# Memory values multiplied by the output weights ahead of the attention, 1/Z moved into the residual addition, and the down projection's first loads moved

## The chip, the cores and the metric

The kernel runs on one core of a Trainium2 chip. Its time is the device time of one execution in microseconds (us); the median of several runs counts. The engines are TensorE (PE, matrix products), VectorE (DVE), ScalarE (ACT) and GpSimd (POOL); SyncE (SP) issues all DMA transfers of this kernel, in one order.

## What is computed

One decoder layer on 1024 tokens of width 1024 in fp32: retention and differential attention side by side, a shared output projection, a cross-attention on 256 memory tokens with 4 heads of 256, and a SwiGLU feed-forward part with 2816 hidden columns. The change concerns the cross-attention and the end of the feed-forward part. The cross-attention in short, with the memory already normalised:

```python
k, v = split(rms_norm(mem, norm_mem) @ xkv)        # 4 heads of 256 each
q = rms_norm(rms_norm(x, norm_x) @ xq, xq_gain)    # per head
p = softmax(q @ rms_norm(k, xk_gain).T / sqrt(256))
x = x + concat_heads(p @ v) @ xo
h = rms_norm(x, norm_ffn)
out = x + (silu(h @ w_gate) * (h @ w_up)) @ w_down
```

## The kernel before

Every product of two fp32 matrices is made of three matmuls of rounded parts: `mm3` takes a high and a low part of each operand and leaves out low times low. So each 128x1024 piece of weights ("unit") is loaded into a stage buffer (`st_...`, three buffers in the pool `raw`, 512 KB each), cast by ACT into a high part (`uh_...`), and the rest is computed by POOL or DVE into a low part (`ul_...`, function `low`). The parts lie in a ring of slots that PE gives back when it has used them.

The work runs in stages: retention and differential attention; the memory's keys and values (`xkv`, eight quarters c of 256 columns, of which 0 to 3 are keys and 4 to 7 the values of heads 0 to 3, evacuated to `kn` and `vx`); the output projection `wo`; the cross-attention loop; a transition, in which normalised rows `xn_f` are transposed (`bt`) for the feed-forward part; gate and up columns j = 0 to 21 by a scheme of seven products (forms, `x`, `y`, `z`, `G`, `U`); and the down projection by seven products again, each in eleven groups p of twelve 128x512 matmuls (`dx`, `dy`). For a group the left operand comes from `gF_d`, where the gate/up results were stored, the right one from the weights or, summed, from `wT_d`; both halves land in one stage buffer `ds`, are cast to `dh` by ACT and split into `dl` by DVE.

The cross-attention loop has 16 steps n (head n // 4, a pair of 128-token tiles n % 4). In a step PE makes scores `xs` of step n, queries `xq` of step n+1, transposes the probabilities `xp` (`xpt`), multiplies the result of step n-1 by the output weights (`xo`, 24 matmuls), sums the squares of the queries with a matmul by ones (`xss`) and multiplies probabilities by values (`xot`). Between these, ACT and DVE compute rsqrt of the query norms, the maximum, exp, 1/Z and the products with it. When the head changes, the weights of the next one are loaded, cast and split by POOL.

A scheduler sets the order of DVE, ACT, POOL and SP from the program's order; PE follows the program. In the gate/up loop the orders of DVE and ACT are those of the program too (`pin`).

Of the kernel before, what the change touches and what calls it, by code (L numbers as in the profile page):

```python
# [37 lines left out]
def body(ctx, tc, a, out):  # L38
# [74 lines left out]
    def unit(i, name, eng=None, pool=None, heng=None, stage=raw, pin=False):  # L113

        st = stage(f"st_{name}")
        sp.dma_start(st, a["w"][i])
# [27 lines left out]
    def rsqrt(ss, n, mean, name):  # L144
# [4 lines left out]
        ve.tensor_scalar(out=xh, in0=ss, scalar1=-0.5 * mean, scalar2=-0.5 * EPS, op0=ALU.mult, op1=ALU.add)  # L149
        ve.tensor_scalar(out=ss, in0=ss, scalar1=mean, scalar2=EPS, op0=ALU.mult, op1=ALU.add)  # L150
# [137 lines left out]
    mix_d = drp.tile([KB, P, S], F32, tag="mix", name="mix_d")  # L288
    mixT = [None, None]
# [304 lines left out]
    class Mem:  # L594
        def __init__(self):
# [18 lines left out]
            self.vx = kv8("vx")  # L614
            self.ssk = small(8, "ssk", "ssk")
            self.u = {}
# [4 lines left out]

        def gemm(self, c, i):
            t, h = divmod(i, 2)
            if i == 0:
                self.load(c + 2)
            if h == 0:
# [3 lines left out]
            mm3(ps[:, 0:256], [((self.h[k // 4][:, b(k)], self.l[k // 4][:, b(k)]), cols(self.u[c], k, 256))  # L630
                               for k in range(4 * h, 4 * h + 4)], start=h == 0, stop=h == 1)
            if h == 0:
                return
            dst = (self.kn if c < 4 else self.vx)[:, t, 256 * (c % 4):256 * (c % 4) + 256]
            sc.activation(dst, ps[:, 0:256], AF.Copy, scale=self.rm[:, t:t + 1])
            if c < 4:
                sq = h1(f"ksq{c}_{t}")
# [126 lines left out]
    kn, vx = mem.kn, mem.vx  # L764
# [10 lines left out]

    def add_res(t, c, ps):
        sl = xr[t][:, 512 * c:512 * c + 512]
        ve.tensor_tensor(out=sl, in0=ps, in1=sl, op=ALU.add)
# [93 lines left out]
    def head(h):  # L872
        uq = [unit(U_XQ + 2 * h + i, f"xq{h}_{i}") for i in range(2)]
        uo = [unit(U_XO + 2 * h + i, f"xo{h}_{i}") for i in range(2)]
        vh = tp4.tile([P, 2, 2, 256], F32R, tag="t4", name=f"xv{h}")
        vsl = vx[:, :, 256 * h:256 * h + 256]
        sc.copy(vh[:, :, 0, :], vsl)
        low(gp, vh[:, :, 1, :], vsl, vh[:, :, 0, :])
        hd[h] = [uq, uo, vh, None]

    def head_k(h):
# [11 lines left out]
        hd[h][3] = kT  # L893
# [12 lines left out]
    def xG(n):  # L906
# [12 lines left out]
        ve.tensor_tensor(out=sq[:, 0:256], in0=sq[:, 0:256], in1=sq[:, 256:512], op=ALU.add)  # L919
        st[n] = [qT, sq]  # L920

    def xR(n):
        qT, sq = st[n]
        sp_ = ms(f"xss{n}")
        for e in range(2):
            pe.matmul(sp_[:, e:e + 1], sq[:, e * P:e * P + P], ones[:, 2:3], start=True, stop=True)
        rq = small(2, "rq", f"rq{n}")
        ve.tensor_copy(rq, sp_[:, 0:2])
        rsqrt(rq, 2, 1.0 / 256, f"q{n}")
        st[n] = [qT, rq]  # L930

    def xS(n):
        h, p = divmod(n, 4)
        qT, rq = st[n]
        kT = hd[h][3]
# [13 lines left out]
        ve.tensor_tensor(out=two(pr), in0=two(pr), in1=bc(Z, 256), op=ALU.mult)  # L949
        st[n] = pr  # L950

    def xT_(n):
        pr = st[n]
# [5 lines left out]
        st[n] = part2(f"xpT{n}", two(tp))  # L959

    def xO(n):
        pT, vh = st[n], hd[n // 4][2]
        ot = ms(f"xot{n}")
        for i in range(2):
            mm3(ot[:, 256 * i:256 * i + 256],
                [((vh[:, mt, 0, i * P:i * P + P], vh[:, mt, 1, i * P:i * P + P]), (pT[:, mt, 0, :], pT[:, mt, 1, :]))
                 for mt in range(2)])
        st[n] = part2(f"xoT{n}", two(ot))

    def xX(n, parts=range(4), mm=mm):  # L970
        h, p = divmod(n, 4)
        oT, uo = st[n], hd[h][1]
        for e, c in [divmod(i, 2) for i in parts]:
            t = 2 * p + e
            ps = mm(f"xo{n}_{e}_{c}")
            mm3(ps, [((oT[:, i, 0, e * P:e * P + P], oT[:, i, 1, e * P:e * P + P]),
                      cols(uo[i:i + 1], 0, 1024, 512 * c, 512)) for i in range(2)])
            add_res(t, c, ps)
            if h == 3 and c == 1:
                sp.dma_start(res_d[t], xr[t])  # L980
                xns.append(normed(t, hd["g"], f"f{t}"))
                if e:
                    b_sums(p)
# [7 lines left out]
    for n in range(15):  # L991
# [18 lines left out]
        xO(n)  # L1010
# [141 lines left out]

    c0, c1, call_ = slice(0, 256), slice(256, 512), slice(0, 512)
# [5 lines left out]
    xO(15)  # L1159
# [27 lines left out]
    for j in range(NH):  # L1187
        n, c = None, c1 if j == 0 else call_
        if j % 2 == 0:
            w_load(j // 2)  # L1190
# [6 lines left out]
        if n:  # L1197
            fn.form(6)
            fn.form(3)
        o.after(7, c)  # L1200
# [5 lines left out]
        if n and fm:  # L1206
            fm.form(1)
# [12 lines left out]
        if j % 2:  # L1220
            g_forms(j // 2)
        if n:
# [5 lines left out]
    res = [bp.tile([P, 2, D], F32, tag="B", bufs=4, name=f"res{t}") for t in range(4)]  # L1228
    res = [res[t // 2][:, t % 2] for t in range(NT)]
    for t in range(NT):  # L1230
        sp.dma_start(res[t], res_d[t])
# [3 lines left out]
    gsrc = {1: (0, 0), 2: (1, 0), 4: (1, 1), 5: (2, 0), 6: (2, 1), 7: (3, 0), 3: (3, 1)}  # L1235
    wsrc = {5: (0, 0), 7: (0, 1), 4: (1, 0), 6: (1, 1)}
# [3 lines left out]
    h5_ = lambda i: slice(512 * i, 512 * i + 512)  # L1240
    for f in (1, 2, 6, 5, 7, 3, 4):
        bank = Y if f in (2, 5, 3) else X
# [112 lines left out]
```

## Time and profile before

| | us |
|---|---|
| median of 3 runs (1640.39 to 1641.12) | 1640.43 |
| profiled execution | 1642.59 |
| its span on the core | 1640.8 |
| PE busy | 1547.2 (94%) |
| DVE busy | 1046.6 (64%) |
| ACT busy | 616.3 (38%) |
| POOL busy | 283.1 (17%) |

The span reaches from the first to the last instruction; the execution's time is measured around it. Busy shares are means over stages that have different limits.

### The profile page before, as it was taken

Reading aid. Unit: us, or ns where it says so; the run is one execution under the profiler, and the core shown is the slowest. Engines: PE = TensorE matmul, PEld = TensorE weight load, DVE = VectorE, ACT = ScalarE, POOL = GpSimd, SP = SyncE. Lnnn points to the kernel's source line nnn. Section 1 sums busy time; section 2 is a strip of 40 time slices with the busy share of each in tenths; the row PEclk is TensorE's granted clock in tenths of the full one; section 3 lists DMA queues with packets and bytes.
Section 4 is the critical chain, followed back from the end, with each engine's and each line's share of the span. In section 5 each row is a group of like instructions: output and inputs, shape, how many; then the busy total and the mean of one; then the engine's idle time right before and its main releaser. Section 6 shows DMA issues by size and latency. Waiting matters only on the chain.

```text
span 1640.8 us, 23170 instructions
## 1 busy us (share of the span) xinstructions
PE 1547.2 (94%) x8712; PEld 1321.6 (81%) x8712; DVE 1046.6 (64%) x2578; ACT 616.3 (38%) x1187; POOL 283.1 (17%) x238
## 2 busy tenths in 40 slices
PE   5899899999999989999999979999999999899998
PEld 5778878878877978799899858788888888688887
DVE  8864873873876543756666886666666666455554
ACT  4442442442444731333223353333333333243332
POOL 4323222222212331102112230010000000000000
PEclk9899999999999999999999989999999999999999
DMA  8201110110102562101101122444444444766564
GB/s 286 71 27 39 34 51 27 44 52 26 39 27 97 187 217 84 46 1 39 39 27 39 65 103 84 148 148 147 148 161 147 168 163 171 255 215 219 195 218 154
DMA packets 68079, 180.82 MB, mean 110 GB/s; under 512 B 7296, under 2 KB 12800, under 8 KB 67968
## 3 DMA queue, kind: packets, MB, share of 16 engines
q1 hardware_dynamic: 66960, 178.81, 30.8%
q8 instruction: 68, 1.11, 0.3%
q10 hardware_dynamic: 1008, 0.55, 0.1%
q14 instruction: 43, 0.35, 0.1%
HBM read 135.55 MB, written 43.78 MB: 109 GB/s over the span
## 4 chain that ended last, share of the span: by engine, by line
PE 75%; DVE 16%; ACT 3%; DMA 3%; issue 1%; POOL 1%; SPq 0%; ACTq 0%; DVEq 0%; POOLq 0%
PE x L64 14%; PE g_r L64 8%; PE z L64 7%; PE dx L64 7%; PE dy L64 5%; PE wo L64 5%; PE xo L64 5%; PE xq L64 4%; PE y L64 3%; PE kv L64 3%; PE q L64 2%; PE av L64 2%; DVE dsm L52 2%; DVE rw_d L52 2%; DVE nmx L52 1%
## 5 line engine op out<-in xcount | busy, mean ns | idle before, releaser
L64 PE MATMUL g_r<-uh_r,xT 128*128 128x512 f32 x512 | 178.2, 406 | 0.0
L52 DVE TENSOR_TENSOR dl<-ds,dh 128x1024 fp32r<-128x1024 f32 x77 | 94.2, 1224 | 98.0 <-PE dy L64 36.6
L52 ACT CAST dh<-ds 128x1024 fp32r<-128x1024 f32 x77 | 81.2, 1054 | 133.1 <-DMA ds<-in_w_dram 41.5
L64 PE MATMUL kv<-uh_d,xT 128*128 128x256 f32 x512 | 112.4, 302 | 6.2 <-DVE dql L52 6.2
L64 PE MATMUL x<-Bh,f 128*128 128x512 f32 (+1 forms) x368 | 114.6, 383 | 1.5 <-DVE G L52 1.4
L64 PEld LDWEIGHTS g_r<-uh_r,xT 128*128 128x128 f32 x512 | 96.4, 188 | 22.3 <-issue 2.5
L52 DVE TENSOR_TENSOR f<-s,f 128x512 fp32r<-128x512 f32 x86 | 65.0, 756 | 62.8 <-ACT f L52 62.8
L52 POOL TENSOR_TENSOR G<-G,U 128x512 f32<-128x512 f32 (+1 forms) x23 | 35.6, 1549 | 399.2 <-DVE U L52 381.3
L64 PE MATMUL g_r<-ul_r,xT 128*128 128x512 f32 x256 | 100.6, 393 | 0.0
L64 PEld LDWEIGHTS kv<-uh_d,xT 128*128 128x128 f32 x512 | 88.3, 200 | 8.7 <-DVE dql L52 6.4
L64 PE MATMUL xq<-hT,uh_xq 128*128 128x256 f32 x512 | 94.3, 286 | 0.0
L52 ACT CAST f<-s 128x512 fp32r<-128x512 f32 x88 | 54.6, 620 | 104.2 <-DVE s L52 102.5
L64 PE MATMUL xo<-uh_xo,xoT 128*128 128x512 f32 x256 | 90.2, 412 | 2.1 <-DVE B6l L52 1.6
L52 ACT ACTIVATE p<-s,nmx,dsm 128x128 f32<-128x128 f32 (+7 forms) x64 | 53.2, 832 | 98.6 <-DVE nmx L52 95.3
L64 PEld LDWEIGHTS x<-Bh,f 128*128 128x128 f32 x368 | 69.2, 191 | 15.2 <-DVE G L52 2.1
L64 PEld LDWEIGHTS xq<-hT,uh_xq 128*128 128x128 f32 x512 | 81.0, 195 | 0.0
L64 PE MATMUL kv<-ul_d,xT 128*128 128x256 f32 x256 | 74.8, 292 | 1.9 <-DVE ul_d L52 1.9
L52 DVE TENSOR_TENSOR f<-gu,f 128x512 fp32r<-128x512 f32 x63 | 43.4, 689 | 49.2 <-ACT f L52 49.2
L64 PE MATMUL dx<-dh 128*128 128x512 f32 x176 | 69.6, 396 | 5.2 <-ACT dh L52 5.2
L64 PE MATMUL xq<-hT,ul_xq 128*128 128x256 f32 x256 | 73.1, 286 | 0.0
L52 DVE TENSOR_TENSOR G<-x,G 128x512 f32<-128x512 f32 (+1 forms) x69 | 45.7, 662 | 41.9 <-ACT G L52 38.5
L64 PE MATMUL x<-Bl,f 128*128 128x512 f32 (+1 forms) x184 | 70.3, 382 | 0.0
(325 smaller groups left out, 4247.1 us busy)
## 6 DMA issues: line engine op xcount, KB each, us to landing
gu<-in_w_dram SPq DMA_DIRECT2D x21, 1024.0 KB, 6.0
ds<-gF_d SPq DMA_DIRECT2D x77, 256.0 KB, 2.9
wd<-in_w_dram SPq DMA_DIRECT2D x22, 512.0 KB, 5.6
wT_d<-wd SPq DMA_DIRECT2D x22, 512.0 KB, 3.0
ds<-wT_d SPq DMA_DIRECT2D x44, 256.0 KB, 3.4
ds<-in_w_dram SPq DMA_DIRECT2D x33, 256.0 KB, 3.3
st_r<-in_w_dram SPq DMA_DIRECT2D x16, 512.0 KB, 3.3
st_kv<-in_w_dram SPq DMA_DIRECT2D x16, 512.0 KB, 3.3
```

The costliest lines, as they stand in the source:

```text
L52: r = f(*args, **kw)
L64: return tc.keep_in_program_order(nc.tensor.matmul(*args, **kw))
```

## The change

It has four parts. (1) The values of a head are computed transposed and multiplied by that head's 256 rows of xo (`vo`), before the output projection; the 256x1024 result is stored in `vo_d` and loaded in place of xo in `head`. The product `xO` of probabilities and values disappears, and `xX` multiplies the probabilities by the stored result. The units of xo are loaded among those of kv; unit 4 of kv is loaded twice. (2) Probabilities stay undivided; 1/Z becomes a factor in the residual addition. The two halves of the query squares are summed by two more ones-matmuls. (3) The rows of a token pair share one rsqrt ahead of the feed-forward part. (4) Loads, casts and low parts of the down projection's first three groups are written into the last gate/up column, the residual's loads after its fourth group; the last product's last three groups run by output tile.

```diff
         def gemm(self, c, i):
+
             t, h = divmod(i, 2)
             if i == 0:
-                self.load(c + 2)
+                self.load(c + 2 if c < 2 else c + 1 if c > 2 else 4)
...
+            if c > 4 and t == 0:
+                self.vo(c - 5, h)
+            if c > 3 and t == 0 and h:
+                self.load_o(c - 4)
             if h == 0:
                 return
...
+            else:
+                v = self.vT[c - 4, t] = [h1(f"vT{x}{c - 4}_{t}", F32R) for x in "hl"]
+                sc.copy(v[0], ps[:, 0:256])
+                low(ve, v[1], ps[:, 0:256], v[0])
...
+        def vo(self, h, mt):
+            v, uo, m = [self.vT[h, i] for i in range(2)], self.uo[h], slice(mt * P, mt * P + P)
+            o = t4(f"vo{h}_{mt}")
+            for c in range(2):
+                ps = ms(f"vo{h}_{mt}_{c}")
+                mm3(ps, [((v[i][0][:, m], v[i][1][:, m]), cols(uo[i:i + 1], 0, 1024, 512 * c, 512))
+                         for i in range(2)])
+                sc.activation(o[:, 512 * c:512 * c + 512], ps, AF.Copy, scale=self.rm[:, mt:mt + 1])
+            sp.dma_start(vo_d[2 * h + mt], o)
...
-        uo = [unit(U_XO + 2 * h + i, f"xo{h}_{i}") for i in range(2)]
-        vh = tp4.tile([P, 2, 2, 256], F32R, tag="t4", name=f"xv{h}")
...
+        uo = [unit(vo_d[2 * h + i], f"vo{h}_{i}") for i in range(2)]
...
-        ve.tensor_tensor(out=sq[:, 0:256], in0=sq[:, 0:256], in1=sq[:, 256:512], op=ALU.add)
...
-            pe.matmul(sp_[:, e:e + 1], sq[:, e * P:e * P + P], ones[:, 2:3], start=True, stop=True)
+            for i in range(2):
+                pe.matmul(sp_[:, e:e + 1], sq[:, 256 * i + e * P:256 * i + e * P + P], ones[:, 2:3],
+                          start=i == 0, stop=i == 1)
...
-        ve.tensor_tensor(out=two(pr), in0=two(pr), in1=bc(Z, 256), op=ALU.mult)
...
-            add_res(t, c, ps)
+            sl = xr[t][:, 512 * c:512 * c + 512]
+            ve.scalar_tensor_tensor(out=sl, in0=ps, scalar=Z[:, e:e + 1], in1=sl, op0=ALU.mult, op1=ALU.add)
...
+                    rsqrt(hd["r"], 2, 1.0 / D, f"f{p}")
...
+        if j == NH - 1:
+            for p in range(3):
+                d_load(1, p, raw if p == 2 else xnp_tile)
...
+        else:
+            d_cast(1, 0)
         o.after(7, c)
...
+            if f == d_order[0] and p == 4:
+                res2 = [bp.tile([P, 2, D], F32, tag="B", bufs=4, name=f"res{t}") for t in range(4)]
+                res = [res2[t // 2][:, t % 2] for t in range(NT)]
+                for t in range(NT):
+                    sp.dma_start(res[t], res_d[t])
+            if (f, p) not in du:
+                d_load(f, p, raw if p % 2 else t4)
+                d_cast(f, p)
```

SP, value stage, before. kv6 and kv7 are units of value quarters 6 and 7, mixs are pieces of the mixed attention output; all of them use the ring of stage buffers, and the numbers at the end of a name count tiles.

```order
L52 DMA mixs1_6596<-mix_d_202 128x1024
L52 DMA st_kv6_0_6649<-in_w_dram 128x1024
L52 DMA st_kv6_1_6655<-in_w_dram 128x1024
L52 DMA mixs6_6713<-mix_d_202 128x1024
L52 DMA g_x_6934<-in_g_x_dram 128x1024
L52 DMA st_kv7_0_6719<-in_w_dram 128x1024
L52 DMA xres_0_0_6985<-in_x_dram 128x512
L52 DMA st_kv7_1_6725<-in_w_dram 128x1024
L52 DMA mixs2_6783<-mix_d_202 128x1024
L52 DMA mixs7_6841<-mix_d_202 128x1024
```

SP, the same place with the change. xo0 and xo1 are the output-weight units of heads 0 and 1, vo_d the stores of the finished product.

```order
L52 DMA st_xo0_0_6693<-in_w_dram 128x1024
L52 DMA st_xo0_1_6699<-in_w_dram 128x1024
L52 DMA mixs6_6738<-mix_d_202 128x1024
L52 DMA st_kv6_0_6744<-in_w_dram 128x1024
L52 DMA st_kv6_1_6750<-in_w_dram 128x1024
L52 DMA vo_d0_203<-vo0_0_6769 128x1024
L52 DMA st_xo1_0_6817<-in_w_dram 128x1024
L52 DMA st_xo1_1_6823<-in_w_dram 128x1024
L52 DMA vo_d1_204<-vo0_1_6799 128x1024
L52 DMA mixs2_6862<-mix_d_202 128x1024
L52 DMA st_kv7_0_6868<-in_w_dram 128x1024
```

Between the units of kv6 and of kv7 there are now two units of xo and two stores.

PE, attention loop, before: the end of step 4, from the sums of squares to the next scores.

```order
L64 MATMUL xss5_8531<-ones_148,xsq5_8493 128x1 x2
L64 MATMUL xo3_1_1_8552<-uh_xo0_0_7660,xoT3_8419 128x512
L64 MATMUL xo3_1_1_8552<-ul_xo0_0_7661,xoT3_8419 128x512
L64 MATMUL xo3_1_1_8552<-uh_xo0_0_7660,xoT3_8419 128x512
L64 MATMUL xo3_1_1_8552<-uh_xo0_1_7666,xoT3_8419 128x512
L64 MATMUL xo3_1_1_8552<-ul_xo0_1_7667,xoT3_8419 128x512
L64 MATMUL xo3_1_1_8552<-uh_xo0_1_7666,xoT3_8419 128x512
L64 MATMUL xot4_8560<-xpT4_8504,xv1_8277 128x256 x12
L64 MATMUL xs5_8576<-xkT1_8396,xqT5_8494 128x256 x12
```

PE, the same place with the change.

```order
L64 MATMUL xss5_8690<-ones_148,xsq5_8653 128x1 x4
L64 MATMUL xo3_1_1_8712<-uh_vo0_0_7895,xpT3_8516 128x512
L64 MATMUL xo3_1_1_8712<-ul_vo0_0_7896,xpT3_8516 128x512
L64 MATMUL xo3_1_1_8712<-uh_vo0_0_7895,xpT3_8516 128x512
L64 MATMUL xo3_1_1_8712<-uh_vo0_1_7901,xpT3_8516 128x512
L64 MATMUL xo3_1_1_8712<-ul_vo0_1_7902,xpT3_8516 128x512
L64 MATMUL xo3_1_1_8712<-uh_vo0_1_7901,xpT3_8516 128x512
L64 MATMUL xs5_8720<-xkT1_8573,xqT5_8654 128x256 x12
```

The product xot is gone, xo takes the probabilities xpT and the units uh_vo and ul_vo, and the ones-matmul stands four times.

DVE, end of the gate/up stage, before. wd10 are the sums of down weights for the last pair of groups, G21 and U21 the last column's results, gSa a sum of results.

```order
L52 TENSOR_TENSOR wd10_1_13664<-wd10_1_13664,wd10_0_13663 128x512
L52 TENSOR_TENSOR wd10_1_13664<-wd10_1_13664 128x512
L52 TENSOR_TENSOR G21_13726<-x21_13667,G21_13726 128x512
L52 TENSOR_TENSOR U21_13755<-x21_13667,U21_13755 128x512
L52 TENSOR_TENSOR G21_13726<-x21_13667,G21_13726 128x512
L52 TENSOR_TENSOR gSa10_13821<-G20_13585,G21_13726 128x512
```

DVE, the same place with the change.

```order
L52 TENSOR_TENSOR wd10_1_13571<-wd10_1_13571 128x512
L52 TENSOR_TENSOR G21_13633<-x21_13574,G21_13633 128x512
L52 TENSOR_TENSOR dl1_0_13723<-ds1_0_13701,dh1_0_13722 128x1024
L52 TENSOR_TENSOR U21_13662<-x21_13574,U21_13662 128x512
L52 TENSOR_TENSOR dl1_1_13741<-ds1_1_13704,dh1_1_13740 128x1024
L52 TENSOR_TENSOR G21_13633<-x21_13574,G21_13633 128x512
```

The low parts dl1_0 and dl1_1 of the down projection's first two groups now stand among the last column's additions, dl1_0 ahead of U21.

## Rows read from the trace of the kernel before

**Rows 1.** Chain of waits, 728 to 746: start us, us, engine, tile, line, count.

```profile
729.13 1.43 PE xot L64 x12
...
732.00 5.76 PE xq L64 x48
...
738.20 4.13 PE xo L64 x18
742.33 0.34 PE xss L64 x4
```

**Rows 2.** Waits of PE in 560 to 600: us in total, times, longest.

```profile
PE xkv L64 <- ACT vx L52: 4.1, 2, 2.2
PE mt L68 <- DVE ro L52: 1.7, 1, 1.7
PE wo L64 <- POOL ul_wo L52: 1.4, 1, 1.4
```

**Rows 3.** Timeline, 554 to 578: POOL and PE; last bracket: idle before.

```profile
554.65 2.39 POOL L52 TENSOR_TENSOR ul_kv<-st_kv,uh_kv 128x1024 fp32r<-128x1024 f32 x1 [5.09 <-ACT uh_kv L52]
...
561.97 0.36 PE L64 MATMUL xkv<-uh_kv,memTh 128*128 128x256 f32 x1
...
569.53 3.49 POOL L52 TENSOR_TENSOR ul_kv<-st_kv,uh_kv 128x1024 fp32r<-128x1024 f32 x1 [4.68 <-ACT uh_kv L52]
```

**Rows 4.** Chain of waits, 561 to 600.

```profile
595.64 4.38 PE wo L64 x18
```

**Rows 5.** Groups by form, 560 to 600: busy us, mean ns, idle before.

```profile
L52 ACT CAST uh_kv<-st_kv 128x1024 fp32r<-128x1024 f32 x5 | 5.2, 1042 | 6.9 <-DMA st_kv<-in_w_dram 6.9
...
L52 DVE TENSOR_TENSOR ul_kv<-st_kv,uh_kv 128x1024 fp32r<-128x1024 f32 x3 | 3.7, 1220 | 3.4 <-ACT uh_kv L52 3.4
```

**Rows 6.** The page, part 6: DMA issues, KB each, us to landing.

```profile
st_kv<-in_w_dram SPq DMA_DIRECT2D x16, 512.0 KB, 3.3
```

**Rows 7.** Timeline, 774 to 786: POOL, DVE and PE.

```profile
774.33 4.78 POOL L52 TENSOR_TENSOR ul_xo<-st_xo,uh_xo 128x1024 fp32r<-128x1024 f32 x2 [26.23 <-issue]
...
774.52 2.25 DVE L52 TENSOR_SCALAR ry_q<-rq 128x2 int32<-128x2 int32 x1
...
784.19 0.69 DVE L52 TENSOR_TENSOR xp<-xp,xZ 128x512 f32<-128x512 f32 x1
...
785.03 0.63 PE L68 MATMUL xpt<-ident,xp 128*128 128x128 f32 x4 [1.30 <-DVE xp L52]
```

**Rows 8.** Waits of PE in 700 to 940.

```profile
PE xpt L68 <- DVE xp L52: 5.4, 4, 1.9
```

**Rows 9.** Waits of PE in 940 to 1010.

```profile
PE bt L68 <- DVE xn_f L52: 6.9, 2, 5.2
PE bt L68 <- DVE ry_f L52: 2.6, 1, 2.6
```

**Rows 10.** Chain of waits, 1405 to 1445.

```profile
1414.04 0.70 DVE U L52
...
1414.88 3.00 PE x L64 x12
...
1425.31 7.50 DMA ds<-in_w_dram
...
1435.27 9.85 PE dx L64 x32
```

**Rows 11.** Timeline, 1405 to 1437: DMA issues of SP, casts of ACT.

```profile
1408.34 1.77 SPq L52 DMA_DIRECT2D wT_d<-wd  x2
...
1410.78 0.32 SPq L52 DMA_DIRECT2D ds<-gF_d  x1
...
1416.52 1.05 ACT L52 CAST dh<-ds 128x1024 fp32r<-128x1024 f32 x1 [4.92 <-DMA ds<-in_w_dram]
```

**Rows 12.** Busy time by stretch: span, engines, then TensorE clock, DMA share, GB/s.

```profile
1410.00:1430.00 20.00, 16.98 (x72) 13.28 (x72) 7.89 (x10) 4.00 (x5) 1.29 (x1) 1.00 0.97 340
1430.00:1440.00 10.00, 5.53 (x12) 4.05 (x13) 3.68 (x3) 3.13 (x3) 0.00 (x0) 0.67 0.62 212
```

More of the change, by code (lines that the diff above doesn't have):

```diff
@@ L115, in unit @@
         st = stage(f"st_{name}")
-        sp.dma_start(st, a["w"][i])
+        sp.dma_start(st, a["w"][i] if isinstance(i, int) else i)
         if pool is ntp_[0] and pool is not None:
@@ L142, in mmf, with rsqrt @@
             pe.matmul(ps, l, r, start=i == 0, stop=i == n - 1)
-    def rsqrt(ss, n, mean, name):
+    def rsqrt(ss, n, mean, name, src=None):
+        src = ss if src is None else src
         xh = small(32, "rs_x", f"rx_{name}")[:, :n]
@@ L288, in body @@
     mix_d = drp.tile([KB, P, S], F32, tag="mix", name="mix_d")
+    vo_d = [drp.tile([P, D], F32, tag=f"vo{i}", name=f"vo_d{i}") for i in range(8)]
     mixT = [None, None]
@@ L620, in load, with load_o @@
                 self.u[c] = [unit(U_KV + 2 * c + i, f"kv{c}_{i}", eng=ve if i else gp, pool=up if i else uqp, pin=c < 1) for i in range(2)]
+        def load_o(self, h):
+            self.uo[h] = [unit(U_XO + 2 * h + i, f"xo{h}_{i}", eng=ve if i else gp) for i in range(2)]
         def gemm(self, c, i):
@@ L763, in body @@
             run_fin(True)
-    kn, vx = mem.kn, mem.vx
+    for t in range(2):
+        mem.vo(3, t)
+    kn = mem.kn
     p1.close()
@@ L958, in xT_ @@
                              pr[:, 256 * e + mt * P:256 * e + mt * P + P], ident)
[L959 to L968, printed above, removed]
+        st[n] = [part2(f"xpT{n}", two(tp)), Z]
     def xX(n, parts=range(4), mm=mm):
         h, p = divmod(n, 4)
-        oT, uo = st[n], hd[h][1]
+        (pT, Z), uo = st[n], hd[h][1]
         for e, c in [divmod(i, 2) for i in parts]:
@@ L1158, in body @@
     o.go(1, c0)
-    xO(15)
     o.go(2, c0)
@@ L1199, in body @@
             fn.form(3)
+        else:
+            d_cast(1, 0)
         o.after(7, c)
@@ L1205, in body @@
         o.prod(4, c)
-        if n and fm:
+        if not n:
+            d_cast(1, 1)
+        elif fm:
             fm.form(1)
@@ L1221, in body @@
             g_forms(j // 2)
+        if not n:
+            d_cast(1, 2)
         if n:
@@ L1226, in body @@
     pin[0] = False
[L1228 to L1231, printed above, removed]
+    res = []
     xs_ = [s2(f"dx{i}") for i in range(2)]
@@ new lines, in d_out @@
+    def d_out(f, i):
+        for b_, e, c, *last in outs[f]:
+            t = 2 * i + e
+            dst = res[t][:, h5_(c)]
+            add(ve, dst, b_[i], dst)
+            if last:
+                sp.dma_start(out[t][:, h5_(c)], dst)
+    for f in d_order:
+        for p in range(NP):
+            if f == d_order[0] and p == 4:
[6 more added lines that the diff above has]
+                d_cast(f, p)
+            if f != d_order[-1] or p < NP - 3:
+                for i in range(4):
+                    d_prod(f, p, i)
+        if f == d_order[-1]:
@@ L1255, in body @@
             for i in range(4):
-                sl = slice(P * i, P * i + P)
-                mm3(bank[i], [((hi[:, sl], lo[:, sl]), (hi[:, 512:1024], lo[:, 512:1024]))],
-                    start=p == 0 and f in (1, 2, 5), stop=p == NP - 1, skip_group_check=f not in (1, 2, 5))
-        for b_, e, c, *last in outs[f]:
+                for p in range(NP - 3, NP):
+                    d_prod(f, p, i)
+                d_out(f, i)
+        else:
             for i in range(4):
-                t = 2 * i + e
-                dst = res[t][:, h5_(c)]
-                add(ve, dst, b_[i], dst)
-                if last:
-                    sp.dma_start(out[t][:, h5_(c)], dst)
+                d_out(f, i)
```

92 lines of the change are left out of this document (52 added, 40 removed).

## The prediction

> **What bounds the kernel now.** The page comes first: TensorE (PE) is busy for nearly all of the span (the table of times has it), so time is won only by less PE work or by PE waits that disappear, and each stage has to be read for its own waits. I read, in this order, the chain of waits of a step of the memory attention, the waits of PE stage by stage, the timelines around those waits, and the end of the gate/up stage.
>
> In the attention loop PE runs without a gap: xot 1.43 us, xs, 48 xq matmuls in 5.76, the softmax's transposes xpt, 18 xo matmuls in 4.13, and xss 0.34 [rows 1]. A 128x256 matmul thus costs 0.12 us and a 128x512 one 4.13/18 = 0.229. The loop loses 5.4 us, in four waits of xpt for the softmax [rows 8]. In the stage that makes the memory values PE waits 4.1 + 1.7 + 1.4 = 7.2 us, for the evacuation vx, for ro and for a weight's low part [rows 2]; it begins at 561.97 [rows 3] and the output projection runs freely from 595.64 [rows 4]. From there back to 561.97 are 33.7 us.
>
> **The change, part by part.**
>
> *Value stage.* Added on PE: 96 matmuls of 128x512, 96 x 0.229 = 22.0 us. The transposed value product keeps its 48 matmuls of 128x256 per quarter. If nothing else bound, the 22.0 would first fill the 7.2 of waits: +14.8 is the lower end. But each xo unit now has to be loaded, cast and split here. The order of SP shows the ring of three stages: the load of kv6_0 waits for the low part of xo0_0 on POOL, xo1_0's for that of kv6_0, kv7_0's for that of xo1_0. Each such link costs an issue of 0.32 [rows 11], 3.3 to landing [rows 6], a cast of 1.04 [rows 5] and a POOL low of 2.39 [rows 3]: 7.05 us. A value quarter has two links, 14.1 us, while its PE work is 48 x 0.12 + 24 x 0.229 = 11.3. So I take the ring as the bound of quarters 5, 6 and 7. The stage is then quarter 4 (5.8) + 3 x 14.1 + vo(3) (24 x 0.229 = 5.5) + the low of wo0_2, which needs a slot that vo(3) frees last (2.4) = 56.0 us, against 33.7: **+22.3**. The upper end is what happens if lows and VectorE (DVE) operations hold each other up: the low that took 2.39 in a quiet stretch took 3.49 at 569.53 [rows 3]. Six links at 1.1 more are +6.6, so +28.9.
>
> By the Trainium skill (SBUF — State Buffer, Who interferes with whom) a DVE instruction with two SBUF inputs contends with a GpSimd instruction that reads SBUF. The row at 569.53 agrees; by that rule every overlap would cost what the upper end costs, and the sum would be 6.6 higher.
>
> The sixteen evacuations on ScalarE (ACT), the eight stores of vo on SP and the value casts I cost at nothing: ACT has some 11 us per quarter for four casts, four evacuations and two value casts, about 4 x 1.04 + 4 x 0.7 + 2 x 0.5 = 8 (estimates from the cast's 1.04 [rows 5]). If that cover is gone, a cast that stands behind an evacuation lengthens a link, which the upper end includes. The second load of kv unit 4 sits under the last retention head.
>
> *Attention loop.* Per step xot goes (1.43) and xss doubles (0.34 more, bounds 0 and 0.34): -1.09, fifteen times, **-16.4** (to -21.5). The sixteenth xot lies in the transition, under another wait. The four waits of xpt start where POOL's two lows, 4.78 us, hold DVE's rsqrt back: an operation of a few elements takes 2.25 beside them [rows 7]. Behind them the chain loses the multiplication by 1/Z (0.69 [rows 7]), the reciprocal and the low of xoT that stood in DVE's order, about 1.7 together; but PE arrives 1.4 earlier. So 0.3 of each wait goes: **-1.1** (0 to -5.4). The residual addition keeps its count and shape and its 64 operations stay off the chain. The units now come from vo_d instead of the input: same sizes, and same slots.
>
> *Transition.* PE waits 6.9 for the normalised rows and 2.6 for their rsqrt [rows 9]. One joint rsqrt drops seven small operations per pair but the even token's normalisation now waits for the odd one. **-2** (bounds -5 and +2).
>
> *Down projection.* The order of DVE shows what the diff does not say: the low part dl1_0 now stands ahead of the addition U of the last gate/up column, and its load ds1_0, which had landed long before, has moved on SP behind the two stores of wT. These end at 1408.34 + 1.77 = 1410.1 [rows 11]. The next load pair, issued at 1410.78, reached its cast at 1416.52, so 5.7 us later [rows 11], at a DMA share of 0.97 [rows 12]. ds1_0 then lands at about 1415.8, cast and low (1.04 + 1.22 [rows 5]) end at 1418.1, and U at 1418.8 instead of 1414.74 [rows 10]: +4.1 for the last product. Behind U wait the product of 3.00 [rows 10], the last G, its sums and their stores; behind these, on SP, the load of ds1_4. Before, PE ended the product at 1417.88 and the next four groups (48 x 0.229 = 11.0) at 1428.9; that load landed at 1432.81 [rows 10] and its cast ended 1.04 later, so PE waited about 5, and then ran at a mean clock of 0.67 in that stretch [rows 12]: 32 matmuls in 9.85 [rows 10] instead of 32 x 0.229 = 7.3, 2.5 lost. Now PE gets through its first four groups 4.1 later, at about 1432.8; ds1_4 issues some 3 later (dl1_1 no longer stands among the sums) and travels 4 to 7.5 us in a queue that has had time to empty. PE resumes between 1433 and 1437 and loses little or none to the clock: **-1** (bounds -3.4 and +4.1).
>
> The regrouped last product can bring its additions forward by little; I take nothing for it.
>
> **Sum.** 22.3 - 16.4 - 1.1 - 2 - 1 = +1.8 us on the profiled execution's 1642.59, 1644.4; that execution lies 2.2 above the median of the runs, so 1640.43 + 1.8 = **1642.2**. PE does as much as before (23.0 of xot out; 22.0 of vo and 5.4 of xss in), so the change is decided by waits.
>
> **The rivals.**
> 1. *The value stage takes the work into its gaps* (faster). If loads run ahead, the stage costs 14.8 instead of 22.3: 1634.7. For it: PE waits 7.2 there already, and no single row shows the ring full. Against it: three stages, and twice as many units. It decides once a link falls below 11.3/2 = 5.7 us.
> 2. *Contention lengthens the links* (slower). Six links at 3.49 instead of 2.39: 1648.8. For it: 569.53 [rows 3] and the 2.25 us operation [rows 7]. Against it: the low at 554.65 was undisturbed. The Trainium skill's rule named above is this case.
> 3. *The last gate/up column waits and nothing is given back* (slower): ds1_4 lands as late behind its issue as before, +4.1 instead of -1: 1647.3. For it: share 0.97 [rows 12].
> 4. *The waits of xpt vanish* together with a shorter xss: 3 to 9 off, 1633 to 1639; it needs POOL's lows to move away from the rsqrt, and the order keeps them there.
>
> **Chances.** Forecast 0.40 (its own range 1638 to 1648), rival 1 0.20, rival 2 0.22, rival 3 0.12, rival 4 0.06. The range takes rivals 1 to 4 and a little of their combinations: 1631 to 1652. 0.2% is 3.3 us, about what a measurement of this kernel can tell from no change. Below 1637.1 lie rival 1, most of rival 4 and some of the forecast's lower half: 0.28. Within, the middle of the forecast and the edges of the rest: 0.33. Above 1643.7: 0.39.
>
> **What would show it.** In the profile after: the stretch from the first value matmul to the output projection's free run, 56 us (48.5 by rival 1, 62 by rival 2), with PE waiting there for ul_xo or ul_kv lows on POOL; attention steps 1.09 shorter, with xpt still waiting at the change of heads; U of the last column waiting for dl1_0; and a shorter wait of dx for its fifth group. I am wrong if PE is gapless in the value stage, if U starts at its old distance from G, or if the steps are not shorter, because the ones-matmuls or the additions from PSUM cost more than their rows say.

## The result and the profile after

The changed kernel takes 1659.95 us (median of 4 runs, 1658.47 to 1663.66), the one before 1640.41 on the same chip: 1.0129 times as long, 95% interval 1.0109 to 1.0148. The forecast, 1642.2 within 1631 to 1652, was wrong. The profiled span went from 1640.8 to 1658.7 us.

The start and end times of the tiles cut the span into stretches. The later runs are read by stretches too, since whole times of one kernel differ by several us from run to run (the kernel before: 1635.8 to 1645.3 in all runs).

| stretch, us | before | forecast | after |
|---|---|---|---|
| value stage: first value product to second `wo` product | 33.7 | 56.0 | 63.1 |
| to the first `xs` | 107.4 | 107.4 | 107.4 |
| attention loop: to the last `xs` | 236.3 | 218.8 | 219.0 |
| transition and gate/up: to the last `y` | 458.6 | 456.6 | 460.7 |
| to the first `dy` | 58.6 | 57.6 | 62.4 |
| down projection: to the last `dy` | 149.4 | 149.4 | 149.4 |
| tail: to the end | 34.9 | 34.9 | 36.2 |

Only the loop came out as forecast; every other stretch that the change touches is longer than forecast.

PE's waits in the value stage of the changed kernel, 555 to 630 (us in total, times, longest), to hold against [rows 2]:

```profile
PE xkv L64 <- DVE vTl L52: 4.8, 1, 4.8
PE vo L64 <- POOL ul_xo L52: 1.8, 2, 1.4
PE wo L64 <- POOL ul_wo L52: 1.5, 1, 1.5
PE vo L64 <- ACT vo L52: 1.4, 1, 1.4
PE vo L64 <- DVE ul_xo L52: 1.2, 2, 0.8
```

The waits did not fill up; they grew, 7.2 us before and 10.7 in these rows. The longest is on none of the tiles that the forecast named. Busy times of the stage, before and after (span, PE, PEld, DVE, ACT, POOL, clock, DMA share, GB/s; 1.00 is the upper of TensorE's two clock levels, 2.4 GHz, and a value below it a mean in which part of the stretch ran at 1.2):

```profile
561.97:595.64 33.67, 26.57 (x203) 25.61 (x203) 25.45 (x43) 18.37 (x30) 16.92 (x6) 0.95 0.59 201
```

```profile
560.47:623.56 63.09, 51.13 (x300) 43.17 (x299) 38.39 (x58) 38.80 (x57) 25.43 (x10) 0.95 0.70 243
```

Of the 29.4 us, PE is at work for 24.6 more and idle for 4.9 more. The waits of SP in 560 to 625 show the forecast's ring, and something longer:

```profile
SPq L52 <- ACT vo L52: 15.6, 8, 5.1
SPq L52 <- POOL ul_xo L52: 9.8, 3, 3.6
SPq L52 <- POOL ul_kv L52: 8.1, 3, 3.6
```

Loads did wait for POOL's lows, but in SP's one order they also stood behind the stores of `vo`, which wait for ACT's evacuations.

The timelines of POOL, DVE and PE around PE's longest wait (start, us; in brackets the idle time before):

```profile
567.21 2.35 POOL L52 TENSOR_TENSOR ul_xo<-st_xo,uh_xo 128x1024 fp32r<-128x1024 f32 x1 [1.88 <-ACT uh_xo L52]
567.43 2.15 DVE L52 SCALAR_TENSOR_TENSOR ry_kx<-rw_kx,ry_kx 128x8 f32<-128x8 f32 x1
569.50 1.21 DVE L52 TENSOR_TENSOR ul_kv<-st_kv,uh_kv 128x1024 fp32r<-128x1024 f32 x1
570.79 0.41 DVE L52 TENSOR_TENSOR vTl<-xkv,vTh 128x256 fp32r<-128x256 f32 x1
571.26 0.58 PE L64 MATMUL xkv<-memTh,uh_kv 128*128 128x256 f32 x1 [4.82 <-DVE vTl L52]
```

`vTl` reads the PSUM tile that PE wants next. It stands behind the key norm's small operations, one of which, on eight elements a row, ends with POOL's low (567.43 + 2.15 = 569.58, 567.21 + 2.35 = 569.56), and behind a low of DVE itself. Before, that PSUM tile was emptied by ACT.

In the loop (728 to 950) the waits of [rows 8] are nearly gone:

```profile
PE xs L64 <- ACT xkT L52: 1.7, 3, 0.6
PE xpt L68 <- ACT xp L52: 0.9, 2, 0.6
```

Of the transition, waits in 948 to 1025, to hold against [rows 9], and the busy times of one stretch:

```profile
PE bt L68 <- DVE xn_f L52: 8.2, 2, 5.8
PE bt L68 <- DVE Bl L52: 3.8, 2, 2.4
```

```profile
970.00:990.00 20.00, 11.80 (x57) 10.16 (x57) 14.62 (x27) 8.53 (x15) 9.06 (x6) 0.71 0.35 131
```

The chain of waits from the last gate/up column into the down projection, to hold against [rows 10]:

```profile
1422.58 5.44 DMA ds<-in_w_dram
...
1428.09 1.05 ACT dh L52
...
1429.16 0.40 DVE dl L52
...
1430.31 0.69 DVE U L52
...
1431.14 5.12 PE x L64 x12
...
1443.13 6.75 DMA ds<-in_w_dram
...
1452.33 9.81 PE dx L64 x34
```

U waits for the low `dl`, this for a load, as forecast. But the product behind U takes 5.12 us where it took 3.00, and the later load is awaited again. The chain in the tail shows the regrouped last product:

```profile
1646.68 0.70 DVE res L52
...
1647.43 4.41 PE dx L64 x18
...
1651.86 0.70 DVE res L52
...
1652.61 2.38 PE dx L64 x9
```

PE waits for an addition twice: the outputs of two token tiles are halves of one PSUM tile, so the product into one half waits until the other has been read.

### The profile page after: what moved, and what is told of

Same layout as the page of the kernel before. It is cut to its first block, busy times and chain, and to the rows that moved or that the text cites. A ratio compares the mean times of both kernels' runs of the same rounds, so it can differ in the third digit from the quotient of the medians.

```text
span 1658.7 us, 23025 instructions
## 1 busy us (share of the span) xinstructions
PE 1559.6 (94%) x8680; PEld 1325.3 (80%) x8680; DVE 1021.6 (62%) x2499; ACT 624.6 (38%) x1193; POOL 289.2 (17%) x239
## 5 line engine op out<-in xcount | busy, mean ns | idle before, releaser
L52 ACT CAST dh<-ds 128x1024 fp32r<-128x1024 f32 x77 | 81.1, 1055 | 134.7 <-PE dy L64 53.3
L52 POOL TENSOR_TENSOR G<-G,U 128x512 f32<-128x512 f32 (+1 forms) x23 | 35.3, 1535 | 404.0 <-DVE U L52 393.3
L64 PE MATMUL xo<-uh_vo,xpT 128*128 128x512 f32 x256 | 88.9, 406 | 0.1
```

What stands on the lines that cost most here:

```text
L52: r = f(*args, **kw)
L64: return tc.keep_in_program_order(nc.tensor.matmul(*args, **kw))
```

## The experiments

"Value part" is from the last evacuation of `kn` to the first `xs`: 140.7 us before, 168.2 in the changed kernel. "The stage" is from the first value product to the second `wo` product, 33.7 and 63.1. One profile was taken of each run, and stretches of the same code differ between them: the stage 62.0 to 63.1 us and the value part 167.2 to 168.7 in the changed kernel, x1, x7, x8 and x11; in the three runs with the value stage of before (before, x4, x12) 33.4 to 33.8 and 140.7 to 143.2; last `xs` to last `y` 460.2 to 462.0 in the 15 runs with the joint rsqrt, last `y` to first `dy` 60.7 to 63.6 in the 14 with all of part 4. Ratios are to the kernel before, run on the same chip; 1.0129 is that of the change.

**x1_old_down**: the down projection as before (loads, order, residual and last product).

```diff
-            for p in range(3):
-                d_load(1, p, raw if p == 2 else xnp_tile)
...
-            d_cast(1, 0)
```

> The changed kernel with the down projection of the kernel before (its loads, casts, residual loads and last product). Theory 1 (the end loses time because dl1_0 holds U of the last column back, and because the regrouped last product waits for its own additions): 5.1 us less than the changed kernel's 1660, so about 1655; from the last y matmul to the first dy matmul 58.6 us again instead of 62.4, and from the last dy to the end 34.9 instead of 36.2. Rival (the end is slow through something that the earlier stages hand on, such as the clock or DMA traffic): both stretches keep 62.4 and 36.2, and the time stays at 1660.

1.0083 [1.0054, 1.0112]; the time itself, 1659.0 us, shows little of the 5.1 expected. Last `y` to first `dy` 58.7 us for 62.4, tail 35.3 for 36.2. Part 4 of the change is a loss of 4.6 us by these stretches (of 3 to 6 by the spread named above).

**x8_cast_after_u**: only the first of the moved conversions goes behind the last U.

```diff
-            d_cast(1, 0)
         o.after(7, c)
...
+            d_cast(1, 0)
             d_cast(1, 1)
```

> The changed kernel with the first conversion of the down projection's weights (p 0 of the first product) written after the last U product of the gate stage instead of ahead of it. Theory A (DVE runs dl, 1.2 us, ahead of U, so that x waits 4.2 us for U and the clock falls to 0.71 behind the wait): x<-U falls below 1.5 us, the last y to the first dy goes from 62.4 us to 57-59, and the time falls by 3-5 us. Rival B (dh and dl are awaited by the first down product instead): dx<-dh or dx<-dl grows by 3 us or more and the stretch stays at 61-63 us.

1.0110 [1.0081, 1.0138]. The stretch is 59.6 us. Of PE's waits in 1400 to 1480 two tell it:

```profile
PE dx L64 <- ACT dh L52: 6.3, 1, 6.3
...
PE x L64 <- DVE U L52: 0.9, 1, 0.9
```

The wait for U fell from 4.2 to 0.9, that for `dh` rose from 3.9 to 6.3, and 2.8 of the 3.8 us came back: mostly A. The rows show the mechanism; the size is less sure, as x2 and x3, which leave this part as in the change, have 60.7 us. The granted clock in 1425 to 1435 was 1.00 here and 0.70 in the changed kernel.

**x4_invz_only**: the kernel before with the division in the residual addition, nothing else.

```diff
-        ve.tensor_tensor(out=two(pr), in0=two(pr), in1=bc(Z, 256), op=ALU.mult)
...
-            add_res(t, c, ps)
+            ve.scalar_tensor_tensor(out=sl, in0=ps, scalar=Z[:, e:e + 1], in1=sl, op0=ALU.mult, op1=ALU.add)
```

> The kernel before with one thing of the change: probabilities stay undivided and 1/Z becomes a factor in the residual addition (rsqrt reads PSUM directly too; the query squares are still added by DVE, xot stays). Theory 3 (DVE's part of the softmax is what the four waits of xpt, 5.4 us together, consist of): these waits fall to 1.5 us or less and the time by about 4 us to 1636.5. Rival (the division is hidden in three of four steps, and the rsqrt held by POOL sets those waits): the waits stay above 4 us, and the time within 1 us of 1640.4.

0.9974 [0.9964, 0.9983]: faster than before. The loop is 231.2 us for 236.3; the wait of `xpt`, 5.4 us in [rows 8], is 1.1:

```profile
PE xpt L68 <- ACT xp L52: 1.1, 4, 0.5
```

The division, one half of part 2, is a gain by itself, though last `xs` to last `y` is 461.0 us for 458.6.

**x7_sq_add**: the squares added on DVE again, two ones-products a step for four.

```diff
+        ve.tensor_tensor(out=sq[:, 0:256], in0=sq[:, 0:256], in1=sq[:, 256:512], op=ALU.add)
```

> The changed kernel with the sum of the two squared halves made on DVE again, and two ones-products a step instead of four. If the two added products of a step (some 0.17 us each) lie on TensorE's path, the loop from the first to the last xs goes from 219.0 to 212-215 us and the time falls by 4-6 us. Rival: the DVE addition brings xss later by as much as it saves, and xss<-DVE waits of 3 us or more in sum show up: 218-221 us.

1.0096 [1.0067, 1.0126]; the loop is 216.4 us for 219.0. The added ones-products cost 2.6 us net, half of what was forecast; 1.7 us of wait for the DVE addition stand against them.

**x11_norm_apart**: the rows ahead of the feed-forward part normalised one by one.

```diff
+                xns.append(normed(t, hd["g"], f"f{t}"))
```

> The changed kernel with the rows of the feed-forward normalised one by one again, as before, and not in pairs. Theory A (the joint rsqrt makes the even token wait for the odd one, and TensorE waits 8.2 us for xn_f and 3.8 for Bl): the last xs to the last y goes from 460.7 us to 457-459. Rival B (it costs nothing; the version of before with 1/Z alone had 461.0 too): 460-462 us, with waits on xn_f, ry_f and bs of 10 us or more in sum.

1.0109 [1.0085, 1.0133]; last `xs` to last `y` is 458.1 us for 460.7: A by the stretch, though the whole time shows nothing of it. x16, with the rows one by one too, has 459.1. The waits in 948 to 1025 add up to the same, 15.7 us for 15.8 (15.8 to 17.9 in the other runs with the joint rsqrt); the longest is 4.4 for 5.8, and the stretch that answers to the one of the changed kernel with clock 0.71 has 0.83:

```profile
972.20:992.20 20.00, 13.68 (x71) 11.45 (x70) 16.01 (x36) 9.57 (x17) 7.94 (x6) 0.83 0.34 132
```

But the joint rsqrt is not the whole of it: x4 and x12 normalise one by one, wait 16.1 and 16.7 us there, at most 4.3 at once, and still take 461.0 and 460.5. The same stretch in x4:

```profile
955.40:975.40 20.00, 12.40 (x66) 10.38 (x65) 14.38 (x26) 8.85 (x16) 9.86 (x6) 0.74 0.34 127
```

**x3_ring5**: two more stage buffers, for the xo units alone.

```diff
+    xop = p1.enter_context(tc.tile_pool(name="xop", bufs=2))
...
+                               stage=lambda n: xop.tile([P, 1024], F32, tag="xs", name=n)) for i in range(2)]
```

> The changed kernel with two stage buffers of their own for the output-weight units, so that kv, mixed output and wo have the three old ones to themselves. Ring theory (each load waits for the low part of a unit before it): the value stage falls from 63.1 to 56 us or less and the time to about 1653. Theory 2 (DVE's queue at the start): the stage stays at 60 us or more and the wait of xkv for vTl at 4 us or more.

1.0137 [1.0112, 1.0162]; value part 173.8 us, the stage 66.8. SP's waits for POOL's lows of xo and kv fell from 17.9 to 7.4 us in 560 to 625, and the stage became longer: the ring of three, on which the forecast's quarters rested, is not by itself what bounds them. SP's one order stays a bound that this run does not take away: its waits for ACT's `vo` rose from 15.6 to 26.7 us.

**x6_two_ahead**: kv units two columns ahead as before, kv4 loaded once.

```diff
-                self.load(c + 2 if c < 2 else c + 1 if c > 2 else 4)
+                self.load(c + 2)
```

> The changed kernel with the lookahead of before for the value weights (two columns ahead, kv4 loaded once and not twice). If the second load of kv4 and its two conversions cost something at the head of the stage, kn to the second wo product goes from 60.8 us to 56-59. Rival: the second load is hidden and the later loads come no earlier than they are needed: 60-62 us. Other rival: units two ahead hold the stage buffers that the output-weight units need, and the waits on ul_xo and ul_kv grow by 2-5 us: 62-66 us.

1.0162 [1.0127, 1.0196]; value part 176.9 us. The wait for `vTl` grew to 10.6 us, not those for `ul_xo`, and kn to the second `wo` product is 68.5 us: a miss for all three.

**x2_keynorm_late**: the key norm written after the third value column.

```diff
-            if c == 3:
+            if c == 6:
                 rsqrt(self.ssk, 8, 1.0 / 256, "kx")
```

> The changed kernel with the normalisation of the keys (a chain of small DVE operations and two large ones) written after the seventh quarter instead of after the fourth. Theory 2 (the value stage loses its extra time at its start, where DVE's queue of small operations, held up by POOL's low parts, keeps the value's low part vTl waiting, PE stops for 4.8 us and its clock drops): the stage, 63.1 us in the changed kernel, falls to 55 to 58, and the time to about 1654. Rival (the ring of three stage buffers, as the prediction had it): the stage stays at 61 to 63 and the time at 1658 to 1660.

1.0103 [1.0088, 1.0118]; value part 167.1 us. The wait for `vTl` went from 4.8 to 1.1, but `vo` then waited for `ul_xo` (2.9), `vTl` (2.7) and `mix` (1.6). The stage is 61.0, not 55 to 58: the wait went and most of the time stayed.

**x5_xo_low_dve**: all lows of xo on DVE.

```diff
-eng=ve if i else gp
+eng=ve
```

> The changed kernel with the low halves of all eight output-weight units subtracted on DVE instead of four of them on POOL. Theory A (the 4.8 us that TensorE waits for vTl at 571 us comes because DVE's operations of a few elements are held while POOL runs a low of 2.35 us beside them, 1.54 and 2.15 us each): the wait xkv<-DVE vTl falls to 1.5 us or less, kn to the second wo product goes from 60.8 us to 56-58, the time falls by 3-5 us. Rival B (DVE's chain is late because of its own work, and gets four lows of about 1.2 us more): the wait stays at 4 us or more and the stage is 60-64 us long. Rival C (the waits move, as when the key norm was written later): the stage is 59-61 us with the waits on other tiles, their sum still 10-12 us.

1.0136 [1.0107, 1.0164]; value part 168.6 us; the wait for `vTl` 8.9, by B. Of A this clears only the lows of xo; ahead of `vTl`, at 575.62, a small operation is still held beside POOL, now by the retention's `rg`:

```profile
572.18 3.43 POOL L52 TENSOR_TENSOR rg<-rg,ro 128x1024 f32<-128x1024 f32 x1 [6.04 <-DVE ry_kx L52]
573.31 2.32 DVE L52 TENSOR_TENSOR rw_kx<-ry_kx 128x8 f32<-128x8 f32 x1
```

**x15_vo_later**: x2 with `vo` half a column later.

```diff
-            if c > 4 and t == 0:
+            if c > 4 and t == 1:
                 self.vo(c - 5, h)
```

> The changed kernel with each vo half a column later (beside the second half of the rows of a column in place of the first) and the key norm written after the third value column. If the wait behind the first value column lies on DVE's burst alone, the wait xkv<-vTl and the waits of the first vo fall from 7 us in sum to 2 or less, and kn to the first xs goes from 168.2 us to 163-165. Rival (the ring's pace holds the stage whatever the head does): the waits come back in the later columns, 167-170.

1.0129 [1.0100, 1.0159]; value part 168.5 us. The rival: waits come back elsewhere, 2.5 of them on the retention's `mt` behind an evacuation of `vo`.

Five ways of taking a wait away had won at most 1.1 us of the value part, no more than the spread. Two runs then took one side of the stage out each.

**x9_vo_one_product**: `vo` with high parts only.

```diff
-                mm3(ps, [((v[i][0][:, m], v[i][1][:, m]), cols(uo[i:i + 1], 0, 1024, 512 * c, 512))
+                mmf(ps, [(v[i][0][:, m], cols(uo[i:i + 1], 0, 1024, 512 * c, 512)[0])
```

> The changed kernel with one product instead of three for each pair of vo: the products with the low halves are left out, so the memory values lose accuracy; all loads, casts and lows stay. 64 matmuls of 128x512 are gone, 64 x 0.213 to 0.229 = 13.6 to 14.7 us of TensorE's work. Theory A (TensorE's own work and few waits make the stage): kn to the second wo product goes from 60.8 us to 46-49 and the time falls by 12-15 us. Rival B (the supply of weights makes it, as my forecast had it with its ring of 14.1 us a quarter): the stage stays at 56-61 us and TensorE's waits grow by about what the products gave up. Between them: some of the work freed is waited away, 50-55 us.

1.0128 [1.0107, 1.0149]; value part 168.0 us for 168.2. Two thirds of the added PE work left, and nothing was won up to the first `xs`. The stage itself is 59.4 us, 3.7 shorter, near B; most of that is lost again by the first `xs`: at the start of the `wo` products the granted clock is 0.86 (619 to 639), in the changed kernel 1.00 (623 to 643). Waits of this run in 555 to 630, then the busy times of 590 to 620 in it and in the changed kernel:

```profile
PE xkv L64 <- DVE vTl L52: 7.7, 2, 4.7
PE vo L64 <- ACT uh_xo L52: 5.1, 3, 2.6
PE wo L64 <- ACT uh_wo L52: 2.7, 1, 2.7
```

```profile
590.00:620.00 30.00, 21.25 (x115) 17.55 (x114) 10.71 (x15) 20.68 (x31) 12.00 (x5) 0.85 0.86 306
```

```profile
590.00:620.00 30.00, 26.60 (x154) 22.06 (x154) 13.39 (x15) 20.01 (x29) 9.58 (x4) 1.00 0.79 266
```

PE works 5.4 us less there, waits instead, for weights too, and its clock falls from 1.00 to 0.85.

**x10_vo_no_load**: no xo units; `vo` takes kv units that lie in SBUF.

```diff
-            if c > 3 and t == 0 and h:
-                self.load_o(c - 4)
...
-        v, uo, m = [self.vT[h, i] for i in range(2)], self.uo[h], slice(mt * P, mt * P + P)
+        v, uo, m = [self.vT[h, i] for i in range(2)], self.u[min(h + 5, 7)], slice(mt * P, mt * P + P)
```

> The changed kernel without the output-weight units of the value stage: vo takes the value weights that lie in SBUF at that time in their place, so the eight loads, casts and lows are left out and the output is that of other weights; TensorE's work is unchanged. Theory A (TensorE's work makes the stage, the units add waits of 5 to 8 us): kn to the second wo product goes from 60.8 us to 53-57. Rival B (supply makes it): it goes to 48 us or less, all gaps but those of before gone, since 33.3 + 22.0 of work - 7.2 of waits is 48. Rival C: the waits on vTl and vo stay without the units: 58-61 us.

1.0090 [1.0070, 1.0111]; value part 160.9 us, kn to second `wo` product 53.3: A. The wait for `vTl` is still 4.1. The busy times of the stage:

```profile
559.82:615.40 55.58, 49.94 (x299) 43.64 (x299) 30.96 (x55) 31.93 (x49) 16.72 (x7) 0.94 0.59 195
```

PE is at work 23.4 us longer than before, in a stage that is 21.9 us longer.

**x13_loads_only and x14_casts_only** put the transfers or the conversions back into x10.

```diff
+                    sp.dma_start(raw(f"st_xo{c}_{j}"), a["w"][U_XO + 2 * (c - 4) + j])
```

```diff
+                    src = self.h[j].bitcast(F32)
...
+                    sc.copy(hi, src)
+                    low(ve if j else gp, lo, src, hi)
```

> x10_vo_no_load with the eight loads of the output-weight units put back into the ring of stage buffers, without their casts and lows; vo still takes the value weights, so the output is that of other weights. In x10 kn to the first xs was 160.9 us, in the changed kernel 168.2. If the transfers and the places that they hold in the ring make the difference: 166-169. If the conversions on ACT, DVE and POOL make it: 160-163.

> x10_vo_no_load with the eight casts and lows put back, made from memory rows that lie in SBUF, so no transfer stands ahead of them; vo still takes the value weights, so the output is that of other weights. If the conversions make the difference between 160.9 and 168.2 us: 166-169. If the transfers do: 160-163. If neither alone does, since it is the chain of load, cast and low behind one another through the ring: both x13 and x14 lie at 160-164.

Transfers alone: value part 161.6 us, 1.0097 [1.0066, 1.0128]. Conversions alone: 171.0, above the 166 to 169 that was expected, 1.0135 [1.0101, 1.0169], with these waits:

```profile
PE xkv L64 <- DVE vTl L52: 6.3, 1, 6.3
PE vo L64 <- DVE vTl L52: 5.9, 2, 3.9
```

PE waits here for values that DVE has not split yet. In front of the second wait DVE is itself held beside POOL: a low that takes 1.2 us alone takes 3.36.

```profile
594.74 2.78 POOL L52 TENSOR_TENSOR ul_xo<-memTh,uh_xo 128x1024 fp32r<-128x1024 f32 x1
595.25 3.36 DVE L52 TENSOR_TENSOR ul_kv<-st_kv,uh_kv 128x1024 fp32r<-128x1024 f32 x1
598.53 0.41 DVE L52 TENSOR_TENSOR vTl<-xkv,vTh 128x256 fp32r<-128x256 f32 x1
```

The transfers cost 0.7 us, although the DMA share is 0.73 to 0.92 in 580 to 630 of the changed kernel. x14 starts its conversions without waiting for a load, so it can be worse than the change itself.

**x17_no_lows**: the changed kernel with loads and casts of xo, without its lows.

```diff
+                sc.copy(hi, s_)
+                self.uo[h].append((hi, hi))
```

> The changed kernel without the eight lows of the output-weight units: vo takes the high half in the low half's place, so the memory values lose accuracy; loads, casts, ring and TensorE's matmuls stay. If the lows on DVE and POOL are what the units cost: kn to the first xs goes from 168.2 us to 160-163, as without the units (x10, 160.9), and the time falls by 5 to 8 us. If the casts on ACT are: 166-169.

1.0094 [1.0072, 1.0117]; value part 162.6 us. The lows cost 5.6 of the 7.3 us that the units cost. Without them stage buffers also come free earlier, so this run alone does not tell the engines' time from the ring's; x14, whose conversions take no place in the ring, speaks for the engines.

**x18_lows_on_pool**: all eight lows of xo on POOL.

```diff
-eng=ve if i else gp
+eng=gp
```

> The changed kernel with all eight lows of the output-weight units on POOL (x5 had all on DVE and came out at 168.6 us from kn to the first xs, DVE busy 39.2 us of 563 to 633, as in the changed kernel with 39.4). Theory A (a low on POOL, about 2.4 us, holds DVE about as long as DVE needs to do it, 1.2 us): DVE stays busy 38 to 40 us there and the stretch 167-170. Rival (work taken from DVE is won): DVE 35 us or less, 163-166. Other rival (POOL's lows of 2.4 us become the chain that vo waits for): 170 or more, with vo waiting for ul_xo on POOL for 5 us or more.

1.0168 [1.0140, 1.0195]; value part 176.5 us. Busy times of 563 to 633 in x17, in this run and in the changed kernel:

```profile
563.00:633.00 70.00, 61.91 (x349) 52.59 (x348) 33.41 (x55) 40.05 (x58) 17.66 (x7) 1.00 0.77 268
```

```profile
563.00:633.00 70.00, 54.80 (x296) 46.41 (x295) 35.02 (x52) 39.20 (x57) 35.28 (x15) 0.88 0.66 220
```

```profile
563.00:633.00 70.00, 58.04 (x320) 48.45 (x320) 39.43 (x57) 38.05 (x56) 28.11 (x11) 0.95 0.71 247
```

DVE is busy 35.0 us here (though still all of 570 to 580), so A falls; but the stretch is 8.3 us longer, with waits for `ul_xo` (3.0, fewer than the 5 expected) and `vTl` (6.8): relieving DVE wins nothing here, and by the stretch the last of the three expectations is the nearest. With all lows on DVE (x5) it was 39.2, no more than with half of them on POOL.

**x12_invz_and_tail**: x4 with the regrouped last product, in an order of output tiles that keeps halves of one PSUM tile apart.

```diff
+            for i in (0, 2, 1, 3):
+                for p in range(NP - 3, NP):
+                    d_prod(f, p, i)
+                d_out(f, i)
```

> The kernel before with the division moved into the residual addition (as in x4_invz_only) and with the last down product grouped by output rows, in an order that lets no product wait for the addition of the other half of its PSUM tile (0, 2, 1, 3). Theory A: the loop is 231-232 us as in x4, the last dy to the end goes from 34.9 us to 33-34, and the time lies 4 to 6 us under that of before. Rival B (the grouped product still waits, as in the changed kernel, where this stretch took 36.2): 35-37 us, and the time is that of x4, 0.2 to 0.3% under before, or behind it.

1636.41 us, 0.9971 [0.9961, 0.9982]: the fastest of all. Loop 231.1, tail 33.9 us, and the chain shows the product in one piece:

```profile
1614.95 16.11 PE dx L64 x71
...
1631.08 0.69 DVE res L52
```

Against x4 the gain of 0.7 us in the tail shows in the stretch, not in the time (0.9974).

**x16_all_mended**: x15 with every other miss mended (x1, x7, x11, x12).

```diff
-            if c > 4 and t == 0:
+            if c > 4 and t == 1:
                 self.vo(c - 5, h)
...
+                xns.append(normed(t, hd["g"], f"f{t}"))
...
+            for i in (0, 2, 1, 3):
```

> The changed kernel with everything mended that the runs priced: x15's value stage, the squares added on DVE (x7), the rows normalised one by one (x11), the down projection's head as before (x1), the last product grouped in the order 0, 2, 1, 3 (x12). Kept of the change: values times output weights per head, and the division in the residual addition. If the prices add up: 1660 - 2.6 - 2.6 - 3.7 - 2.3, and 0 to 5 for x15, gives 1644 to 1649, so not faster than before: the value stage's 27 us against the loop's 20. Rival (they overlap): 1650 or more.

1650.05 us, 1.0053 [1.0034, 1.0073]: 1 us above what was expected, and just at the rival's bound of 1650. Value part 167.1 (+26.4 to before), loop 217.4 (-18.9), the stretches behind it 0.3 longer in sum. The prices add up nearly (9.9 us off the change, 11.2 expected without x15), and what is left against before is the value stage.

## Why the prediction was wrong

**The value stage** (+22.3 forecast, +29.4 measured) is the step that failed most. Its three middle quarters took 42.2 us (571.3 to 613.5), as forecast with 3 x 14.1, but that is luck. The ring's links are there, in SP's waits; as the bound of the quarters they are not borne out: with more than half of SP's waits for the lows gone (x3) the stage was longer, and without any xo unit (x10) it still took 55.6 us, nearly the forecast's 56.0. PE's own quarter was put at 11.3 us from rows 1; in x10 a quarter takes 13.0, with PE busy in 37.7 of the 39.1 us of three at a granted clock of 0.94. So the 22 us of new PE work found no gaps, against rival 1: without the units, or without their lows (x17, 56.6), the stage is 22 to 23 us longer than before. The lows add 5 to 7 us, with waits on DVE and POOL, which is near the mechanism of rival 2; I had it as less likely than the ring. What is over the forecast's 56.0 is the wait of 4.8 us behind the first value column, 571.3 - 566.4: I cost the value casts at nothing and checked that cover for ACT only, though the split was moved to DVE, which is busy for 10.0 of the 10 us from 570 to 580. And the last `vo` took 8.3 us (613.5 to 621.8), not 5.5, with waits inside. But neither is a price that can be struck out alone: x2 and x15 removed most or some of the first wait and won 1.1 us or nothing, as the waits behind it grew. The stores of `vo`, also put at nothing, held SP's order for 15.6 us; what that costs PE no run shows.

**The loop** (-17.5 forecast, -17.3 measured) is right in its sum only. The division gave 5.1 (x4), not 1.1: most of the wait of `xpt` went, as in rival 4, although POOL's two lows still ran beside the rsqrt in x4 (4.76 us, two operations of 2.38 and 2.32 us beside them):

```profile
775.56 4.76 POOL L52 TENSOR_TENSOR ul_xo<-st_xo,uh_xo 128x1024 fp32r<-128x1024 f32 x2 [26.23 <-issue]
775.61 2.38 DVE L52 TENSOR_SCALAR rq<-rq 128x2 f32<-128x2 f32 x1
778.03 2.32 DVE L52 TENSOR_SCALAR ry_q<-rq 128x2 int32<-128x2 int32 x1
```

So rival 4's effect came without its condition, that the lows move away. The ones-products cost 2.6 net (x7), not 5.1. Without `xot` the loop fell by 231.2 - 216.4 = 14.8, not by 15 x 1.43 = 21.5; 3.3 of the difference lies in more waits for `xkT`, `xss` and `xpt` (2.6 us in x4, 5.9 in x7), and PE is busy 18.6 us less (228.5 in x4, 210.0 in x7), so 1.43 a step was too high a price. Why it was is open.

**The transition** (-2 forecast, +2.1 measured). The gain did not come: the waits are as long as before in sum (15.7 and 15.8 us, from 2 us ahead of the last `xs` to 75 behind it). The joint rsqrt costs 1 to 4 us (458.1 and 459.1 in x11 and x16, 460.2 to 462.0 with it); I weighed fewer small operations against an even token that waits, and the even token's wait weighed more. That is in part argued: x4 and x12, without the joint rsqrt, are no faster (461.0, 460.5), so what else takes time there stays open.

**The down projection** (-1 forecast, +3.8 measured). That U waits for `dl1_0`, and PE 4.2 us for U, came as said, and the wait for the fifth group did become shorter (5.2 to 3.9). The step that failed is that PE then resumes with little or no loss: the clock falls behind this wait (0.70 in 1425 to 1435), the product takes 2.1 us longer, and the next load is awaited once more.

**The tail** (0 forecast, +1.3 measured). I looked for additions that come earlier, not at which outputs share a PSUM tile.

The forecast's remark that PE does as much as before does not follow from its own terms (27.4 us in, 23.0 out); PE's busy time rose from 1547.2 to 1559.6 us.

These misses, 7.1 + 4.1 + 4.8 + 1.3 and 0.2 of the loop, are 17.5; with the 1.8 of the forecast 19.3, which is what the medians differ by (19.5). The span grew by 17.9, as the time ahead of the value stage was 1.5 shorter in this one profile.

## What to carry to other kernels

Where work moves into a stage, add up each engine's load there, and above all that of the engine that now empties PSUM, before you look at the ring or the queue. In a stage where several engines wait for each other, taking one wait away may win nothing: take a whole side out (all loads, all lows, two thirds of the products) to see who holds it. Look at how far one stretch of unchanged code differs between profiles before you put a price on another. And price a change's parts singly: here half of one part was a gain of 0.3% by itself, under a loss of 1.3%.

## What the runs showed of the hardware

DVE's operations of 8 or 16 elements a row, 0.17 us alone, took 2.15 to 2.38 us beside POOL instructions and ended with them (2.15 at 567.43 in the changed kernel, 2.32 at 573.31 in x5). The Trainium skill (SBUF — State Buffer, Who interferes with whom) says that a DVE instruction with two inputs in SBUF contends with a GpSimd instruction that reads SBUF; the rows above agree. The operations of [rows 7] and of x4 that were held have one input each (2.25, 2.38 and 2.32 us), so two inputs are not needed for it here. The same section says that DMA never contends with a compute engine; x13, 0.7 us for 4 MB of loads, speaks for it.

Work taken from PE in the value stage came back as waits and as clock (x9: 5.4 us less work in 30, clock 1.00 to 0.85). In the transition the time goes with the granted clock of the 20 us that begin 20 us behind the last `xs`: 0.81 to 0.83 where last `xs` to last `y` takes 458.1 to 459.1 us (before, x11, x16), 0.67 to 0.79 where it takes 460.2 to 462.0 (all others). The longest single wait does not tell them apart: 5.2 us before, 4.3 in x4.
